# A hybrid two-layer transformer block: the first norm's order, the gates by chunks of time, and the order around three hand-overs

## The chip, the cores and the metric

The kernel runs on one core of a Trainium2 chip. A core has a matrix engine (TensorE, PE in the profile, with its weight loads as PEld), a vector engine (VectorE, DVE), an engine for activation functions (ScalarE, ACT), a general one (GpSimd, POOL) and a queue that issues most transfers (SyncE, SP). Each of them works through its own instructions in their order and waits on semaphores for the others. Matrix products are summed in PSUM, which has eight banks of 128 x 512 single-precision numbers; everything else lies in SBUF, and DRAM is reached by transfers alone. The metric is the device time of one execution in microseconds (us), lower is better.

## The reference, cut to what matters

1024 tokens `x` (the latents) and 256 tokens `ctx` (the context), both 1024 wide, go through two layers; a vector `c` modulates each norm. Everything is computed in float32.

```python
for layer in range(2):
    mod_l = silu(c) @ ada_w[layer] + ada_b[layer]        # six vectors of 1024
    mod_c = silu(c_ctx) @ ada_w[layer] + ada_b[layer]
    h_l = modulate(x, norm1_g, mod_l, 0)                 # rms_norm * (1 + scale) + shift
    h_c = modulate(ctx, norm1_g, mod_c, 0)
    # layer 0: mLSTM in both directions with gates, and window attention
    # layer 1: grouped attention of the latents over context and latents
    y_c, y_l = ab_mixer(...) if layer == 0 else c_mixer(...)
    x = x + mod_l[2] * y_l
    x = x + mod_l[5] * relu(modulate(x, norm2_g, mod_l, 3) @ w1) ** 2 @ w2
    # the context gets the same in layer 0 alone
```

The mLSTM's gates per head and direction are `log_i` and `log_f = log_sigmoid(.)`. In chunks of 128 steps the kernel needs of them the running sum of `log_f`, the running maximum `m_t`, and from these the decay of the state from chunk to chunk, the weights of the keys and `exp(-m_t)`. The scan over a chunk depends on the chunk before by one number per head only.

## The kernel before

Activations lie with their features on the 128 partitions and the tokens along the free axis, in three token groups: two of 512 latents and one of 256 context tokens (`TGS`). A float32 product is made of three products of halves: each operand is split into a rounded part and its remainder (`split`, L378 on ACT for the first and L379 on DVE or POOL for the second; for normed tokens `hhi`, L369, and `hlo`, L372 or L374), and the three matmuls hi-hi, lo-hi, hi-lo follow each other (L404 to L406 in projections, L569 in the first half of the MLP, L1020 in its second).

**First norm.** `ada_quarter` computes a quarter of the modulation's first 2048 columns: matmuls L244 with the vector `c` as the operand that stands still, then a sum over four partition groups by the matmuls L255 with `asel`. The four quarters alternate with the norm statistics of the three groups (`norm_stats`, squares summed on POOL and DVE, L315, and one matmul L300), the application of norm and modulation (`norm_apply`), and the projections of gates, window keys (L2310) and window values (`heads["v"]`, with weights in `mrv` and `irv`, L404 to L406), which take their feature tiles in the order in which the modulation has them.

**Gates.** `gates` held the 16 gate rows over all 1280 tokens: tiles of 36 partitions x 1280 columns, with four heads forward at partition 0 and four backward, reversed in time, at 32. Two scans (L1187, L1188), the logarithm of the sigmoid on ACT, exponentials of single rows (L1225, L1228), and 20 transposes (L1242) that bring the values to time on partitions. In the program it stands between the setup of the window attention (`swa_setup`: key rotation with L464 to L467 and L478) and the context's keys.

**The MLP.** The latents' two groups form a 2 x 2 block product in seven products after Strassen's scheme: `pair(b)` runs it for two tiles of hidden features, with the products `A["11"]`, `S1`, `12`, `S2`, `22`, `S3`, `S4`; L581 and L582 (`finish`) apply relu and square, L624 makes sums, and results go to DRAM (`hd`, `hc`, L584 and L600). For the context there are two direct products per pair (`direct`). The first two pairs run in `start()`. PSUM banks are handed out in turn by the list `psp.tags["A"]`. Into the pairs of layer 0 `fill(k)` puts steps of a generator (`filler`), which computes layer 1's modulation: `ada_sums`, DVE sums L209 and L211 over weights loaded at L202, and matmuls L220 over the partitions. The last pair starts `ahead()`, which loads and splits the first operands of the second half, `mlp_out`, through `mlp_feed` (loads L898, sums L943).

**mlp_out.** It takes operand pairs from a queue, one step for each hidden pair `b`, and adds its products into banks 0 to 7: in the first stage ("14") product 1 into banks 0 to 3 and product 4 into banks 4 to 7. After the second step it also loads the tokens saved before (`x<-xs`, L1088). At its end in layer 0 the context's product lies in four banks, is copied out by ACT (L1119) and transposed (L1126); the norm for layer 1 runs as a generator (`norm_steps`), and then `mixer1` splits its first weights and projects keys (`ks`, squares' matmul L1772, rotation L1775) and values.

**What sets the order.** Where nothing else is said, a scheduler places instructions by priority and its own estimates of time. Inside `manual_schedule(engines=...)` the listed engines keep the order in which the code is written.

## Time and profile before

| | |
|---|---|
| time, median of 3 runs | 2866.45 us (2858.58 to 2867.11) |
| the profiled execution | 2866.29 us, of which its span is 2864.5 us |
| mean granted clock of PE | 0.983 |
| PE idle until its first matmul | 14.1 us |
| transfers | 427.87 MB, 149 GB/s in the mean |
| PE busy in 130 to 175 us / in 175 to 250 us | 31.62 of 45 us at clock 0.77 / 73.69 of 75 us at 1.00 |

A row of a timeline gives the start and the length in us, the engine, the line of the code, the operation, the tiles it writes and reads, the shape and how many instructions were merged; in brackets stands the engine's idle time before them and whose result ended it. A row of windows gives, for a stretch, the busy time of each engine with its number of instructions, then the clock that PE was granted (1.00 is full speed), the share of the DMA engines and GB/s. A group row gives busy time, mean duration in ns, and the idle time before. SPq is the queue of SP.

### The profile page before, as it was taken

To read this page: it belongs to the slowest core of one execution; us is meant where nothing else is said; L and a number is where in the kernel's file an instruction comes from. 1 tells how busy PE (TensorE), PEld (TensorE's weight loads), DVE (VectorE), ACT (ScalarE), POOL (GpSimd) and SP (SyncE) were. 2 spreads that over 40 slices of the span, in tenths; PEclk is the share of its full clock that TensorE was granted. 3 is DMA by queue.
4 is the path that set the end of the run, shared out by engine and by line. 5 is a ranking of instruction groups with operands and counts; after the bars stand their busy time and mean duration, and the time that the engine had idled before them with its cause. 6 is when DMAs were issued, how large, how long until landed. Compare 5 with 4: busy or idle time off the path is not lost.

```text
span 2864.5 us, 41088 instructions
## 1 busy us (share of the span) xinstructions
PE 2733.7 (95%) x14806; PEld 2314.0 (81%) x14806; DVE 1996.7 (70%) x3289; ACT 1493.8 (52%) x2624; POOL 1131.6 (40%) x748
## 2 busy tenths in 40 slices
PE   6789999999999999989999998999989999999999
PEld 3678788878788878868878888999988888888877
DVE  5836556567868887756777846888885567766766
ACT  5565554444564334334345645888876555444332
POOL 3431221110227666550000335777776398840000
PEclk9989999999999999999999999999999999999999
DMA  6112224252333466669764720100026245577674
GB/s 232 61 48 95 90 88 145 96 199 89 115 103 126 165 209 214 219 209 339 249 213 156 250 88 32 34 19 27 19 83 209 86 158 195 193 254 269 212 229 155
DMA packets 193965, 427.87 MB, mean 149 GB/s; under 512 B 20960, under 2 KB 46688, under 8 KB 193760
## 3 DMA queue, kind: packets, MB, share of 16 engines
q1 hardware_dynamic: 193760, 425.24, 44.7%
q8 instruction: 116, 1.90, 0.3%
q14 instruction: 89, 0.73, 0.1%
HBM read 322.65 MB, written 102.50 MB: 148 GB/s over the span
## 4 chain that ended last, share of the span: by engine, by line
PE 67%; DVE 13%; DMA 7%; issue 5%; ACT 4%; POOL 2%; SPq 0%; DVEq 0%; POOLq 0%; ACTq 0%
PE psum L1020 15%; PE psum L569 15%; PE psum L404 5%; PE psum L406 5%; PE psum L405 5%; PE psum L1955 4%; PE psum L2141 3%; DMA hhiraw<-in_w 3%; PE psum L1861 3%; DVE W L379 2%; PE psum L1111 2%; DVE F L211 2%; DVE F L624 1%; PE psum L1453 1%; POOL W L379 1%
## 5 line engine op out<-in xcount | busy, mean ns | idle before, releaser
L379 POOL TENSOR_TENSOR W<-F,W 128x512 fp32r<-128x512 f32 (+2 forms) x323 | 522.8, 1634 | 507.8 <-ACT W L378 390.7
L1020 PE MATMUL psum<-W,W 128*128 128x512 f32 x2688 | 617.1, 391 | 8.7 <-DVE W L379 5.2
L1020 PEld LDWEIGHTS psum<-W,W 128*128 128x128 f32 x2688 | 503.9, 188 | 121.4 <-DVE W L379 12.6
L569 PE MATMUL psum<-hhi,W 128*128 128x512 f32 (+1 forms) x1600 | 448.7, 360 | 12.8 <-DVE x L624 5.9
L378 ACT ACTIVATE W<-F 128x512 fp32r<-128x512 f32 (+2 forms) x380 | 274.2, 739 | 264.5 <-POOL F L542 96.9
L569 PEld LDWEIGHTS psum<-hhi,W 128*128 128x128 f32 x1600 | 288.9, 191 | 59.1 <-DVE x L624 7.2
L569 PE MATMUL psum<-hlo,W 128*128 128x512 f32 (+1 forms) x800 | 287.2, 359 | 0.0
L378 ACT ACTIVATE W<-hhiraw 128x1024 fp32r<-128x1024 f32 x98 | 104.0, 1061 | 320.9 <-PE psum L1020 247.3
L404 PE MATMUL psum<-hhi,W 128*128 128x512 f32 (+1 forms) x624 | 232.9, 373 | 6.7 <-DVE F L478 6.7
L406 PE MATMUL psum<-hhi,W 128*128 128x512 f32 (+1 forms) x624 | 227.8, 365 | 0.4 <-POOL W L379 0.4
L405 PE MATMUL psum<-hlo,W 128*128 128x512 f32 (+1 forms) x624 | 227.5, 365 | 0.0
L943 DVE TENSOR_TENSOR hhiraw<-hhiraw 128x512 f32<-128x512 f32 x154 | 104.8, 689 | 118.2 <-DMA hhiraw<-in_w 117.4
L542 POOL TENSOR_TENSOR F<-F 128x512 f32<-128x512 f32 x112 | 170.0, 1518 | 20.4 <-DMA F<-in_w 6.9
L569 PEld LDWEIGHTS psum<-hlo,W 128*128 128x128 f32 x800 | 153.3, 192 | 21.8 <-issue 0.2
L372 POOL TENSOR_TENSOR hlo<-F,hhi 128x512 fp32r<-128x512 f32 (+1 forms) x24 | 27.9, 1165 | 358.8 <-ACT F L371 353.7
L379 DVE TENSOR_TENSOR W<-hhiraw,W 128x1024 fp32r<-128x1024 f32 x98 | 119.6, 1221 | 50.0 <-ACT W L378 49.8
L404 PEld LDWEIGHTS psum<-hhi,W 128*128 128x128 f32 x624 | 119.0, 191 | 27.6 <-DVE F L478 7.1
L406 PEld LDWEIGHTS psum<-hhi,W 128*128 128x128 f32 x624 | 118.7, 190 | 17.9 <-POOL W L379 0.8
L405 PEld LDWEIGHTS psum<-hlo,W 128*128 128x128 f32 x624 | 119.2, 191 | 16.9 <-issue 1.7
L569 PE MATMUL psum<-x,W 128*128 128x512 f32 x504 | 123.5, 389 | 0.0
L581 ACT ACTIVATE F<-F 128x512 f32<-128x512 f32 x82 | 51.2, 625 | 134.7 <-DVE F L624 134.7
L379 DVE TENSOR_TENSOR W<-hloraw,W 128x1024 fp32r<-128x1024 f32 x98 | 119.4, 1219 | 1.6 <-ACT W L378 1.6
(435 smaller groups left out, 6471.5 us busy)
## 6 DMA issues: line engine op xcount, KB each, us to landing
F<-in_w SPq DMA_DIRECT2D x104, 512.0 KB, 4.3
hloraw<-hd SPq DMA_DIRECT2D x90, 512.0 KB, 4.8
hhiraw<-in_w SPq DMA_DIRECT2D x72, 512.0 KB, 3.9
hd<-F SPq DMA_DIRECT2D x142, 256.0 KB, 2.1
hhiraw<-in_w SPq DMA_DIRECT2D x116, 256.0 KB, 5.3
F<-in_ada_w SPq DMA_DIRECT2D x96, 256.0 KB, 3.2
hd<-x SPq DMA_DIRECT2D x90, 256.0 KB, 2.4
F<-in_win SPq DMA_DIRECT2D x33, 512.0 KB, 3.7
```

The costliest lines, as they stand in the source:

```text
L378: nc.scalar.activation(hi, src, AF.Copy)
L379: eng.tensor_tensor(lo, src, hi.bitcast(F32), op=ALU.subtract)
L404: nc.tensor.matmul(ps, sh, mh, start=i == 0, stop=False)
L405: nc.tensor.matmul(ps, sh, ml, start=False, stop=False)
L406: nc.tensor.matmul(ps, sl, mh, start=False, stop=i == n - 1)
L542: add = lambda o, p, q, how: nc.gpsimd.tensor_tensor(o, p, q, op=how)
L569: nc.tensor.matmul(ps, w[i][:, p], B[j][k], start=first and j == 0 and m == 0, stop=last and j == 3 and m == 2)
L943: tt = lambda o, p, q, how: eng.tensor_tensor(o, p, q, op=how)
L1020: nc.tensor.matmul(bank(base + i), A[u][:, p], B[v], start=first and m == 0, stop=last and m == 2)
L1861: nc.tensor.matmul(ps, s[:, c], m[:, j, t0 : t0 + QT], start=j == 0 and i == 0, stop=j == ND - 1 and i == 2)
L1955: nc.tensor.matmul(u.o[:, :QT], v[x], p[y], start=c == 0 and m == 0, stop=c == 2 * NB - 1 and m == 2)
L2141: self.nc.tensor.matmul(ps, x[:, c], y, start=first and m == 0, stop=last and m == 2)
```

## The change

**First norm.** Each quarter's sum over groups takes one matmul in place of two, with the two columns of `asel` added up ahead of time. The context's tokens are loaded behind quarter 2's weights, their squares are summed by matmuls in PSUM, and all eight feature tiles of the context are normed after quarter 3. **Gates.** The gate rows go to DRAM and come back as 128 x 128 tiles: ten chunks x four heads on partitions 0 to 39 forward, 64 to 103 backward. Scans run over 128 columns; what passes between chunks is brought onto one partition row by a matmul (`across`), scanned over 80 numbers and brought back; three transposes remain, and the rows that the recurrence reads (`mr`, `ir`) go through DRAM once more. `gates` moves behind the context's keys and seven steps of the first head's gathering. **MLP.** The turns in which other work goes into `start()`, the bank order after it, the places of `fill`, the order of `ahead` and of `mlp_out`'s first two steps; the last two pairs of each layer keep the written order on all engines. **End of layer 0.** The first weights of `mixer1` are split in `mlp_out`, the keys' ahead of the four copies and the values' behind them; in layer 0 the second half of a feature tile's norm follows one tile later. **mixer1.** The order among the steps of the key groups.

```diff
+        self.asel2 = cp.tile([P, 2], F32, tag="asel2", name="asel2")
+        nc.vector.tensor_tensor(self.asel2, self.asel[:, 0:2], self.asel[:, 2:4], op=ALU.add)
...
-            for u in range(2):
-                nc.tensor.matmul(
-                    pt[:, 2 * i : 2 * i + 2], acc[:, i * P : (i + 1) * P], self.asel[:, 2 * u : 2 * u + 2],
-                    start=u == 0, stop=u == 1,
-                )
+            nc.tensor.matmul(pt[:, 2 * i : 2 * i + 2], acc[:, i * P : (i + 1) * P], self.asel2, start=True, stop=True)
...
+    def apply_first(self, g, rs, layer, which, tp, j, three=True):
+
         nc = self.nc
         t0, n, vv = g
...
+        t = tp.tile([P, 512], F32, tag="nt", name="nt", bufs=self.nt_bufs)[:, :n]
+        sh = self.shift_of(g, layer, which, j)
+        nc.vector.scalar_tensor_tensor(
+            t, self.x[j][:, t0 : t0 + n], self.gs[layer, which][:, j, vv : vv + 1], rs[:, :n],
+            op0=ALU.mult, op1=ALU.mult,
+        )
+        nc.scalar.activation(self.hhi[:, j, t0 : t0 + n], t, AF.Identity, bias=sh)
+        if j % 2 and three:
+            nc.scalar.activation(t, t, AF.Identity, bias=sh)
+        return t
...
+    def apply_second(self, g, layer, which, j, t, three=True):
...
-                turns = iter((1, 1, 1, 1, 1, 1, 4, 4) if ctx else (0, 1, 1, 2, 1, 2, 1, 2))
+                turns = iter((1, 1, 1, 2, 2, 2, 2, 3) if ctx else (0, 1, 1, 2, 1, 2, 1, 2))
...
-                turns = iter((2, 7, 1, 1) if ctx else (1, 1, 1, 1))
+                turns = iter((4, 6, 1, 1) if ctx else (1, 1, 1, 1))
...
-                        one_left(1)
+                        one_left(int(f < 3))
...
-            psp.tags["A"] = [[0, 1, 2, 3, 4, 5, 6] + ([] if ctx else [7]), 0]
+            psp.tags["A"] = [[4, 5, 6, 0, 1, 2, 3] if ctx else list(range(8)), 0]
...
-            if b == NFF // 2 - 1:
-                fill(2)
...
-            if b < NFF // 2 - 1:
-                fill(3)
+            fill(3)
...
+            if filler:
+                yield
+                yield
...
-            yield
-            yield
+            if not filler:
+                yield
+                yield
...
-            pair(b, A, nxt)
+            if b < NFF // 2 - 2:
+                pair(b, A, nxt)
+            else:
+                with self.tc.manual_schedule(engines={E.PE, E.DVE, E.Activation, E.Pool, E.SP}):
+                    pair(b, A, nxt)
...
-                if not (final and not after and b == ns - 1):
+                if stage == 0 and b < 2:
+                    if b == 0:
+                        first_two = [(*w, e, *queue[e]) for w in plan[kind] for e in range(2)]
+                    queue.popleft()
+                    work = first_two[3:] if b else first_two[:3]
+                elif not (final and not after and b == ns - 1):
...
-                    first = b == 0 and not (both and half == R)
+                    first = b + e == 0 and not (both and half == R)
...
-        for (half, i, k), y in zip(parts, ys):
-            nc.scalar.activation(y, bank(k), AF.Copy)
+        wk, wv = self.first_weights
+        wk()
+        with self.tc.manual_schedule(engines={mybir.EngineType.Activation}):
+            for (half, i, k), y in zip(parts, ys):
+                nc.scalar.activation(y, bank(k), AF.Copy)
+            wv()
...
-        for j in range(ND):
-            self.norm_apply(g, ps, layer, which, tp, [j], three)
+        if layer:
+            for j in range(ND):
+                self.norm_apply(g, ps, layer, which, tp, [j], three)
+                yield
+            return
+        t = []
+        for j in range(ND + 1):
+            if j < ND:
+                t.append(self.apply_first(g, ps, layer, which, tp, j, three))
+            if j:
+                self.apply_second(g, layer, which, j - 1, t[j - 1], three)
             yield
...
+        gd = dr.tile([4, 4, T], F32, tag="gd", name="gd")
+        for i in range(4):
+            nc.sync.dma_start(gd[i], gy[32 * i : 32 * i + 4, :])
+        for i in range(4):
+            R = (FW, BW)[i % 2]
+            nc.sync.dma_start((ig, y)[i // 2][R, :], gd[i].rearrange("h (c t) -> (h c) t", t=P))
...
-        nc.vector.tensor_tensor_scan(b, mask, f[R], 0.0, op0=ALU.mult, op1=ALU.add)
-        nc.vector.tensor_tensor_scan(m, f[R], ig[R], 0.0, op0=ALU.add, op1=ALU.max)
-        g = ig[R]
-        nc.vector.tensor_tensor(g, g, b, op=ALU.subtract)
-        nc.vector.tensor_tensor(b, m, b, op=ALU.subtract)
...
+        for R, o in ((FW, slice(None)), (BW, slice(None, None, -1))):
+            nc.vector.tensor_tensor_scan(b[R, o], z[R, :], f[R, o], 0.0, op0=ALU.mult, op1=ALU.add)
+            nc.vector.tensor_tensor_scan(m[R, o], f[R, o], ig[R, o], NEG, op0=ALU.add, op1=ALU.max)
...
+        def across(c):
+
+            ps = psp.tile("G", "gx")[:, :P]
+            nc.tensor.matmul(ps, col[:, c : c + 1].to_broadcast([P, P]), self.ident, start=True, stop=True)
+            return ps
...
+        for i, (x, dst) in enumerate(((Mh, mr), (Ml, mr), (Ih, ir), (Il, ir))):
+            for d, R in enumerate((FW, BW)):
+                w = dr.tile([4, T], F32, tag=f"gd{i}{d}", name=f"gd{i}{d}")
+                nc.sync.dma_start(w.rearrange("h (c t) -> (h c) t", t=P), x[R, :].bitcast(F32))
+                r = 64 * d + 32 * (i % 2)
+                nc.sync.dma_start(dst[r : r + 4, :].bitcast(F32), w)
...
-                mr, ir, cb, tq = self.gates(kp, small, psa, gy)
                 for _ in st[-1](psa, 0, qs):
                     pass
                 self.gps = self.banks(A=(6, 7))
                 heads = [self.gather(wp, tb, ud, h) for h in range(4)]
                 for _ in range(7):
                     next(heads[0])
+                mr, ir, cb, tq = self.gates(kp, small, psa, dr, gy)
...
+    def begin_mixer1(self):
+
+        a, wp = self.a, self.weights_ring((4, 5, 0, 1), (PG, 2 * PG, 0, 0))
+        self.wk, self.wv = [], []
+
+        def keys():
+            self.wk += [self.unit(wp, a["win1"][8 + kv]) for kv in range(2)]
+
+        def vals():
+            self.wv += [self.unit(wp, a["wv1"][:, i * 1024 : i * 1024 + 1024]) for i in range(2)]
+
+        self.first_weights = keys, vals
...
-        wk = [self.unit(wp, a["win1"][NH + kv]) for kv in range(NKV)]
-        wv = [self.unit(wp, a["wv1"][:, i * 1024 : i * 1024 + 1024]) for i in range(2)]
+        wk, wv = self.wk, self.wv
...
-                    for i in (g, g - 1, g, g - 1):
+                    for i in (g - 1, g, g, g - 1):
                         next(ks[i][kv])
             for kv in range(NKV):
+                next(ks[2][kv])
                 vals(TGS[1], (kv,))
-                for _ in range(2):
-                    next(ks[2][kv])
+                next(ks[2][kv])
...
-            if q < 3:
+            if q < 2:
                 k.load_x(a["x"], TGS[q : q + 1], 0)
-                rs[q] = k.norm_stats(TGS[q], tp, ps, "N")
             if q == 0:
+                rs[0] = k.norm_stats(TGS[0], tp, ps, "N")
                 w = [k.unit(wp, a["win0"][u]) for u in (U_G, U_KB)]
                 hl = [kp.tile([P, T], F32R, tag=x, name=x + "v")[:, :PG] for x in ("mr", "ir")]
                 heads["v"] = k.unit(wp, a["win0"][U_VB], place=(k.F[:, 7 * PG : 8 * PG], *hl))
             k.ada_quarter(q, tp, ps)
+            if q == 1:
+                rs[1] = k.norm_stats(TGS[1], tp, ps, "N")
+            if q == 2:
+                k.load_x(a["x"], TGS[2:], 0)
             todo = [(i, 2 * q, 2 * q + 2) for i in range(min(q, 2))]
-            if q < 3:
+            if q < 2:
                 todo.append((q, 0, 2 * q + 2))
-            else:
-                todo.append((2, 6, 8))
+            elif q == 3:
+                todo.append((2, 0, 8))
             for i, j0, j1 in todo:
+                if i == 2:
+                    nps = ps.tile("N", "nps")
+                    for x in k.sum_steps(TGS[2], tp, nps):
+                        pass
+                    rs[2] = k.norm_rms(TGS[2], tp, nps, x)
                 k.norm_apply(TGS[i], rs[i], 0, 1, tp, range(j0, j1))
...
+    k.begin_mixer1()
```

On DVE, in front of the window attention, the rows of the rotation of the context's keys (L464 to L467, L478; names KL, KH are the split keys) before, with the gates' rows of 36x1280 between them:

```order
L1187 SCALAR_TENSOR_TENSOR x_809<-s6f,x_812 36x1280
L464 TENSOR_TENSOR F<-F 128x256
L1188 SCALAR_TENSOR_TENSOR x_810<-x_812,x_807 36x1280
L465 SCALAR_TENSOR_TENSOR F<-psum,F 128x256
L1190 TENSOR_TENSOR x_807<-x_807,x_809 36x1280
L466 TENSOR_SCALAR F<-F 128x256
L1191 TENSOR_TENSOR x_809<-x_810,x_809 36x1280
L467 TENSOR_TENSOR F<-F 128x256
L1196 COPY rmp<-x_810 36x9
L1200 TENSOR_TENSOR x_811<-x_807,x_809 36x1280
L478 SCALAR_TENSOR_TENSOR F<-psum,vec,F 128x256
```

The same five steps now (L475 to L478, L489):

```order
L475 TENSOR_TENSOR F<-F 128x256
L1211 TENSOR_SCALAR x_1102<-x_1102 128x128
L476 SCALAR_TENSOR_TENSOR F<-psum,F 128x256
L1212 SCALAR_TENSOR_TENSOR x_1102<-x_1102 128x128
L477 TENSOR_SCALAR F<-F 128x256
L478 TENSOR_TENSOR F<-F 128x256
L1214 TENSOR_TENSOR x_1102<-x_1102 128x128
L489 SCALAR_TENSOR_TENSOR F<-psum,vec,F 128x256
```

Three rows of the gates, a tenth as wide, stand where six stood. On PE, the place of the last modulation block's matmuls in the last pair of layer 0 (W_103 holds the operand of its second product, before):

```order
L569 MATMUL psum<-hlo,W_103 128x512
L569 MATMUL psum<-hhi,W_103 128x512
L220 MATMUL psum<-ones,F 128x2 x4
L569 MATMUL psum<-hidA,W_103 128x512
L569 MATMUL psum<-hb,W_103 128x512
```

and now, where W_106 is the operand of the third product and the rows of 256 columns are the context's:

```order
L580 MATMUL psum<-hlo,W_106 128x512
L580 MATMUL psum<-hhi,W_106 128x512
L222 MATMUL psum<-ones,F 128x2 x4
L580 MATMUL psum<-hhi,W_105 128x256
L580 MATMUL psum<-hlo,W_105 128x256
```

They have moved past two products of 12 matmuls each. On SP, at the end of layer 0's first half of the MLP, behind the last modulation weights and four loads of the second half (in_w are the second half's weights, hd and hc its hidden features in DRAM, xs the saved tokens), before:

```order
L600 DMA hd_14_6510<-F 128x512
L600 DMA hd_14_6510<-x_7145 128x512
L898 DMA F<-hd_0_6496 128x1024
L898 DMA F<-in_w 128x2x512
L898 DMA F<-hd_1_6497 128x1024
L600 DMA hd_14_6510<-x_7145 128x512 x2
L584 DMA hd_15_6511<-x_7145 128x512
L898 DMA F<-hd_2_6498 128x1024
L584 DMA hc_15_6527<-F 128x256
L1088 DMA x_10165<-xs_114 128x512
L1088 DMA x_10166<-xs_114 128x512
L1088 DMA x_10167<-xs_114 128x512
```

and now:

```order
L611 DMA hd_14_6492<-x_7127 128x512 x3
L1110 DMA x_10153<-xs_116 128x512
L1110 DMA x_10154<-xs_116 128x512
L1110 DMA x_10155<-xs_116 128x512
L1110 DMA x_10153<-xs_116 128x512
L595 DMA hd_15_6493<-x_7127 128x512
L595 DMA hc_15_6509<-F 128x256
L915 DMA F<-in_w 128x512 x2
L915 DMA F<-hd_0_6478 128x1024
L915 DMA F<-in_w 128x512 x2
L915 DMA F<-hd_1_6479 128x1024
L915 DMA F<-in_w 128x512 x2
```

The loads of the saved tokens, which stood behind the first loads of the second half, now stand ahead of them.

More of the change, by code (lines that the diff above doesn't have):

```diff
@@ L1203, in gates @@
[L1203 to L1210 removed]
+        nc.vector.tensor_tensor(f, ln, z, op=ALU.add)
@@ L2280, in first @@
         tp.place("raw", [x[:, :PG] for x in sl[:6]])
-        tp.place("adaacc", cuts(k.F, H, 6 * PG))
+        tp.place("adaacc", cuts(k.F, H, 6 * PG, 6 * PG + H))
         ps = k.banks(N=(0, 1, 2), G=(0, 1, 2), K=(3, 5, 6), D=(4, 7))
```

165 lines of the change are left out of this document (73 added, 92 removed).

## The prediction

> **What bounds the kernel now.** I read the page first, then PE's order of time for its idle stretches, then windows over these stretches for the granted clock. The page says that this is a TensorE kernel:
>
> ```profile
> span 2864.5 us, 41088 instructions
> PE 2733.7 (95%) x14806; PEld 2314.0 (81%) x14806; DVE 1996.7 (70%) x3289; ACT 1493.8 (52%) x2624; POOL 1131.6 (40%) x748
> PE 67%; DVE 13%; DMA 7%; issue 5%; ACT 4%; POOL 2%; SPq 0%; DVEq 0%; POOLq 0%; ACTq 0%
> ```
>
> PE is idle for 2864.5 - 2733.7 = 131 us, 14 of them before its first matmul, so a change that leaves the products alone can win from the other 117 us and from the time at a reduced clock. The stretches of PE that the change touches are these (start, length, what PE ran, and in brackets its idle time before and who ended that):
>
> ```profile
> 54.62 0.70 PE L300 MATMUL psum<-F,ones 128*128 128x256 f32 x2 [1.21 <-DVE F L315]
> 70.97 0.50 PE L2310 MATMUL psum<-hlo,W 128*128 128x512 f32 x1 [0.55 <-POOL hlo L372]
> 73.20 0.39 PE L2310 MATMUL psum<-hlo,W 128*128 128x256 f32 x1 [0.67 <-POOL hlo L372]
> 82.79 1.22 PE L2310 MATMUL psum<-hhi,W 128*128 128x512 f32 x2 [2.07 <-ACT hhi L369]
> 141.92 0.79 PE L404 MATMUL psum<-hhi,W 128*128 128x512 f32 x1 [6.66 <-DVE F L478]
> 153.84 1.12 PE L475 MATMUL psum<-F,blk 128*128 128x512 f32 x2 [0.58 <-ACT F L446]
> 159.23 0.66 PE L1242 MATMUL psum<-ident,x 128*128 128x128 f32 x2 [4.26 <-issue]
> 165.49 0.55 PE L1413 MATMUL psum<-KH,x 128*128 128x256 f32 x1 [1.64 <-DVE small L1246]
> 872.24 0.80 PE L569 MATMUL psum<-hhi,W 128*128 128x512 f32 x1 [5.45 <-ACT F L581]
> 989.56 1.86 PE L220 MATMUL psum<-ones,F 128*128 128x2 f32 x8 [3.73 <-DVE F L211]
> 1242.22 1.87 PE L220 MATMUL psum<-ones,F 128*128 128x2 f32 x8 [8.47 <-DVE F L211]
> 1274.01 0.96 PE L1020 MATMUL psum<-W,W 128*128 128x512 f32 x3 [1.97 <-ACT F L581]
> 1276.18 4.13 PE L1020 MATMUL psum<-W,W 128*128 128x512 f32 x10 [1.21 <-DVE x L624]
> 1676.13 3.31 PE L1126 MATMUL psum<-ident,F 128*128 128x128 f32 x16 [4.38 <-ACT F L1119]
> 1728.37 0.67 PE L1772 MATMUL psum<-F,ones 128*128 128x256 f32 x2 [3.10 <-DVE F L465]
> 1746.71 0.39 PE L404 MATMUL psum<-W,hhi 128*128 128x256 f32 x1 [3.60 <-DVE F L1775]
> ```
>
> A gap costs more than its length. The windows beside them (stretch, its length, busy time of each engine, granted clock, DMA) show half the clock behind each:
>
> ```profile
> 82.00:88.00 6.00, 5.20 (x11) 3.57 (x12) 6.00 (x7) 4.60 (x7) 3.05 (x2) 0.50 0.23 73
> 139.00:147.00 8.00, 5.08 (x13) 4.02 (x14) 7.91 (x8) 6.34 (x9) 3.58 (x3) 0.57 0.25 69
> 156.00:171.00 15.00, 9.89 (x42) 8.20 (x43) 6.31 (x16) 13.07 (x21) 6.29 (x5) 0.54 0.05 17
> 870.00:877.00 7.00, 4.76 (x12) 3.75 (x13) 7.00 (x8) 5.43 (x13) 6.56 (x4) 0.51 0.22 66
> 1238.00:1249.00 11.00, 6.78 (x20) 5.72 (x21) 8.18 (x11) 5.44 (x10) 2.96 (x2) 0.53 0.53 170
> 1276.00:1280.00 4.00, 3.82 (x10) 3.05 (x11) 2.60 (x3) 1.42 (x3) 4.00 (x2) 0.57 1.05 394
> 1747.00:1750.40 3.40, 3.40 (x19) 3.40 (x19) 0.43 (x1) 0.10 (x1) 0.00 (x0) 0.53 0.13 54
> ```
>
> The busy time of such a window times the share of the clock that is missing is lost: 5.08 x 0.43 = 2.2 us in 139 to 147, 9.89 x 0.46 = 4.5 in 156 to 171, 4.76 x 0.49 = 2.3 in 870 to 877, 6.78 x 0.47 = 3.2 in 1238 to 1249, 1.6 in each of the last two. Even the gap of 2.07 us at 80.72 was followed by a clock of 0.50. So I charge about 1.7 us for a gap of 2 to 4 us, on top of it.
>
> The Trainium skill ("TensorE: Matmul & The Clock Gate", Part 1: The HAM clock gate) says that the clock falls back only after at least one idle window of about 3.4 us; the 2.07 us gap does not bear that out as a bound. By that rule the two waits of under 4 us that I add below would cost 3.4 us less, and the sum would be 2824.9 in place of 2828.3.
>
> **The change part by part.** All terms are against the profiled execution's own time, 2866.29 us, which stands 0.16 us under the median shown.
>
> *First norm (40 to 100 us).* The sums over streams take 4 matmuls per quarter where they took 8. Their row, and that of one product with a full clock:
>
> ```profile
> L255 PE MATMUL psum<-asel,F 128*128 128x2 f32 x64 | 9.1, 273 | 1.8 <-DVE F L251 1.7
> 2549.88 10.41 PE L1020 MATMUL psum<-W,W 128*128 128x512 f32 x45
> ```
>
> Half of 9.1 is 4.6 us, of which the first two quarters' share lies in a stretch where PE waits for weights anyway, so 2.3 count. The context's squares move behind quarter 2, and its 48 products of 256 columns go between those of the value projection, so that the waits of 1.21, 0.55 and 0.67 us (2.4 together) have other matmuls in front of them: the value projection's, at 10.41/45 = 0.23 us each, 72 of them. With 2 us of half clock saved that makes 7. What could hide it: the 2.07 us gap stays, since quarter 3's modulation still stands right before the last tiles. Bounds: 2 (only the halved sums) to 10 (the 2.07 gap and its clock too). **7.**
>
> *Gates (120 to 171 us).* DVE worked its 36x1280 rows between the steps of the key rotation, for which PE waited:
>
> ```profile
> 131.06 0.39 DVE L464 TENSOR_TENSOR F<-F 128x256 f32<-128x256 f32 x1
> 131.38 2.81 DVE L1188 TENSOR_TENSOR_SCAN x<-x,x 36x1280 f32<-36x1280 f32 x1
> 141.40 0.47 DVE L478 SCALAR_TENSOR_TENSOR F<-psum,vec,F 128x256 f32<-128x256 f32 x1
> L1242 PE MATMUL psum<-ident,x 128*128 128x128 f32 x20 | 4.1, 354 | 4.3 <-issue 4.3
> L1237 PE MATMUL psum<-x,ident 128*128 128x10 f32 x16 | 2.8, 308 | 0.2 <-ACT x L1228 0.2
> ```
>
> The chain L464 to L478 took 10.8 us of which its own five steps, at 0.39 to 0.47 us, are about 2 us. After, the rows between them are 128x128; the trace has none of those, and by width (a tenth of 1280) one is between 0.15 and 0.3 us. Gone are the gap of 6.66, and the 0.58, 4.26 and 1.64 us behind it, whose releasers are the old gates' transposes and copies: 13.1 us. With them go 2.2 + 4.5 us of half clock. The old gates' matmuls were 4.1 + 2.8 us; the new are six, about 2 us at the same 0.35 each, which saves 5, but most of these ran at half clock and are counted there: 2. I take off 2 for waits of the rotation itself that come out behind them. Sum 13.1 + 6.7 + 2 - 2 = **20**, bounds 12 (the rotation's chain still late by half) and 25.
>
> *Gates' pieces inside the window attention.* The three sums across chunks and three transposes stand in PE's row between the next head's projections, and the chain from the first pair to the third is some 30 small DVE rows and three ACT ones, at 0.2 to 0.3 us 8 to 9 us. PE has 18 products (18 x 0.23 = 4.1 us) and four short ones before it needs the result. That is a wait of up to 4 us and its clock. The 16 transfers of the results stand on SP ahead of gather writes and weight loads, but what they bring is needed only by the chunk recurrence, hundreds of us later. Bounds -10 and 0; nearest to the count of rows: **-4**.
>
> *Bank order behind start() of layer 0.* The 5.45 us at 866.79 waited for a bank that the last context drain (L581) held; after, the first three banks are 4, 5, 6, which are free. 5.45 + 2.3 = 7.8. PE then comes earlier to 985.83, where it waited 3.73 us for DVE's sums L211, and DVE does not come earlier; part returns there. Bounds 1 to 8: **6**.
>
> *Final modulation block and the last two pairs of layer 0.* The gap of 8.47 us at 1233.75 and 3.2 of clock. The matmuls behind it move 24 products of full width later, 24 x 0.23 = 5.5 us, and what the written order does to the block's loads on SP, which stand behind other pairs' stores, I leave between the bounds. Bounds 5.5 and 11.7: **9**.
>
> *Hand-over to the output product in layer 0.* On SP the loads of x, which wait for the last pair's products, now stand before the first loads of the output stage, and the generator that splits its operands starts two steps later. Step 1's operands are due one product after the start (12 x 0.23 = 2.8 us) in place of two. The old wait was 1.97 + 1.21 + 1.6 of clock. One POOL split takes 2.4 us by the row below, a step has two and an addition. I expect a wait of some 6 us plus clock: 5 worse. Bounds -10 to 0: **-5**.
>
> *The same in layer 1*, where there is no gap now. The last split ended at 2552.98, three us after the output products began:
>
> ```profile
> 2543.53 4.79 POOL L379 TENSOR_TENSOR W<-F,W 128x1024 fp32r<-128x1024 f32 x2 [1.81 <-ACT W L378]
> 2548.84 0.62 ACT L581 ACTIVATE x<-x 128x512 f32<-128x512 f32 x1
> 2550.19 2.79 POOL L379 TENSOR_TENSOR W<-F,W 128x1024 fp32r<-128x1024 f32 x1 [1.87 <-PE psum L569]
> ```
>
> The second step is due at 2549.88 + 2.74 = 2552.6, and the written order puts ACT's part of it behind four activations (L581, L582) of 0.62 us, 2.5 us later than now: 2552.98 + 2.5 - 2552.6 = 2.9 us, and 1.7 of clock. Bounds -8 and 0, **-5**.
>
> *Copies out of PSUM at the end of layer 0.*
>
> ```profile
> 1674.05 1.06 ACT L378 ACTIVATE W<-F 128x1024 fp32r<-128x1024 f32 x1 [5.20 <-DMA F<-in_wv]
> 1675.01 2.04 ACT L1119 ACTIVATE F<-psum 128x512 f32<-128x512 f32 x4
> ```
>
> ACT had stood 5.20 us for a value weight's DMA with the four copies queued behind it. Now the copies stand ahead of that split. The gap was 4.38; what is late next are the transposes' own context drain, and the value weights, which come later. Bounds 2 to 6: **5**.
>
> *Keys of the second mixer.* The squares' matmul goes ahead of the next projection, so that DVE's chain starts up to 24 products of 256 columns earlier. Gaps 3.10 + 3.60 and 1.6 of clock, 8.3 in all; bounds 0 (DVE is the bound there) to 8: **5**.
>
> Sum: 7 + 20 - 4 + 6 + 9 - 5 - 5 + 5 + 5 = **38**, so 2866.3 - 38 = **2828.3**, own range 2812 to 2846 (the terms' bounds do not all fall on one side).
>
> **The rivals.**
>
> *The hand-overs take more.* For it: SP, POOL and ACT serve in order, and all three are moved at these places. Against: each engine is busy for less than 70%. At their lower bounds, -10, -8 and -10 for the window attention, and 1 for the bank order: 7 + 20 - 10 + 1 + 9 - 10 - 8 + 5 + 5 = 19, **2847**.
>
> *All gaps close and nothing new opens.* Upper bounds: 10 + 25 + 0 + 8 + 11.7 + 0 + 0 + 6 + 8 = 69, **2797**. Against: the 985 us wait and L1's splits.
>
> *It doesn't do what it says.* DVE remains the bound in front, since it was the releaser of half the gaps, and rotations wait for it in the same order: first norm 2, gates 5, bank order 1, keys 0, hand-overs as in the first rival: 2 + 5 - 10 + 1 + 9 - 10 - 8 + 5 + 0 = -6, **2872**, or within 0.3% (8.6 us, about what a measurement can tell from no change).
>
> *Slower: the round trip through DRAM holds SP's queue.* 24 transfers are added, 12 out and 12 in, and each inbound one waits for its outbound one. Rows of the page:
>
> ```profile
> hd<-F SPq DMA_DIRECT2D x142, 256.0 KB, 2.1
> F<-in_ada_w SPq DMA_DIRECT2D x96, 256.0 KB, 3.2
> ```
>
> If each had to land before the next, 12 x 2.1 + 12 x 3.2 = 64 us would stand ahead of the next heads' weights, and PE would wait for these: 2866.3 - 38 + 64 = **2892**. It decides from 38 + 9 = 47 us on. Against it: the order puts the reads behind five writes, not one by one. [...]
>
> **How the numbers follow.** Forecast 0.62, first rival 0.17, all close 0.08, no effect 0.07, slower 0.06. The range of 8 in 10 takes the forecast, the first rival and half of "all close": 2800 to 2862. Faster by over 0.3%: 0.62 + 0.17 + 0.08 = 0.87; within: 0.07; slower: 0.06.
>
> **What would show it.** In PE's order of time after: no idle time over 1 us before the products that follow the rotated context keys; none behind the last direct context product of layer 0; under 4 us before the final modulation block; new gaps of 3 to 7 us at both hand-overs to the output product, and 2 to 5 us before the third sum across chunks. A loss of the sum's biggest term would show as an idle stretch between 130 and 170 us with DVE as releaser; SP standing in the gates' transfers while PE waits for a weight would prove the last rival.

## The result and the profile after

The changed kernel takes 2829.09 us (median of 4 runs, 2826.91 to 2831.78) against 2864.67 us before (2858.58 to 2867.11): a ratio of 0.988, with a 95% interval of 0.9865 to 0.9896. That is 35.6 us less; the forecast was 2828.3 us. (The kernel before has one run more than in the table above, which moves its median by 1.8 us.) First the page of the profile after, busy times and the chain that ended last:

```profile
span 2825.1 us, 40958 instructions
PE 2716.9 (96%) x14747; PEld 2303.2 (82%) x14747; DVE 1953.8 (69%) x3299; ACT 1474.9 (52%) x2611; POOL 1114.1 (39%) x741
PE 61%; DVE 12%; DMA 6%; issue 5%; ACT 3%; POOL 3%; SPq 0%; DVEq 0%; POOLq 0%; ACTq 0%
```

The span is 39.4 us shorter (the profiled execution is the fastest of the four). PE's idle time fell from 131 to 2825.1 - 2716.9 = 108 us, that is by 22.6 us; its busy time fell by 16.8, since there are 59 matmul rows less and fewer of them run at half clock. The places of the prediction, in PE's order of time after:

```profile
131.52 0.70 PE L486 MATMUL psum<-F,blk 128*128 128x256 f32 x2 [1.58 <-ACT F L452]
143.14 0.50 PE L415 MATMUL psum<-hhi,W 128*128 128x512 f32 x1 [0.50 <-ACT F L1422]
1206.11 0.47 PE L580 MATMUL psum<-hhi,W 128*128 128x512 f32 x1 [1.73 <-DVE x L635]
1211.18 1.05 PE L222 MATMUL psum<-ones,F 128*128 128x2 f32 x8 [2.06 <-DVE F L213]
1234.63 0.79 PE L1037 MATMUL psum<-W,W 128*128 128x512 f32 x1 [4.09 <-ACT W L389]
1238.88 6.55 PE L1037 MATMUL psum<-W,W 128*128 128x512 f32 x17 [3.46 <-POOL W L390]
1246.88 3.47 PE L1037 MATMUL psum<-W,W 128*128 128x512 f32 x14 [1.46 <-POOL W L390]
1637.28 2.00 PE L1152 MATMUL psum<-ident,F 128*128 128x128 f32 x16
2511.44 3.78 PE L1037 MATMUL psum<-W,W 128*128 128x512 f32 x8 [3.06 <-POOL W L390]
```

Between 130 and 171 us no idle stretch exceeds 1.58 us where there had been 6.66 and 4.26. The transposes of the context (L1152) follow the products without a wait. The final modulation block waits 2.06 us where it waited 8.47, but a wait of 1.73 us for DVE, which the kernel before does not have, stands five microseconds ahead of it. In front of the first output products of layer 0 there are three waits, 4.09 + 3.46 + 1.46 = 9.0 us, in place of 1.97 + 1.21; in layer 1 one of 3.06 us is new. The clock in these stretches, by the windows of the profile after:

```profile
130.00:171.00 41.00, 38.97 (x203) 33.28 (x204) 11.60 (x47) 14.99 (x32) 14.06 (x10) 1.00 0.25 81
842.00:849.00 7.00, 7.00 (x34) 5.83 (x33) 7.00 (x6) 4.86 (x12) 7.00 (x6) 1.00 0.21 62
1234.00:1247.00 13.00, 7.46 (x19) 5.29 (x20) 8.12 (x5) 6.72 (x11) 11.83 (x6) 0.62 0.61 204
2504.00:2518.00 14.00, 10.94 (x35) 8.07 (x35) 9.12 (x6) 6.24 (x8) 10.59 (x5) 0.76 0.91 304
```

The front runs at the full clock and PE is busy 38.97 of 41 us; both hand-overs to the output product run at a reduced one (0.62 and 0.76).

**A table by stage** tells more than the whole time. For each kernel I took from PE's order of time when a given product begins or ends: the first product of the window attention's values (`psum<-x,VV`), the 1st, 438th and 1898th product of the MLP's first half (L569, now L580), the 112th and the last of its second half (L1020, now L1037), the end of the context's transposes (L1126, now L1152), and so on. The number is the time between two of them; "again" is a second profile of the changed kernel (run e5, 2830.62 us; it was expected within 2 us of the first at every stage).

| stage, us | before | changed | again | forecast of the difference |
|---|---|---|---|---|
| start to the first window product | 198.84 | 171.36 | 170.71 | -27 |
| to the first product of layer 0's MLP | 611.27 | 613.61 | 617.96 | +4 |
| to its 438th | 93.30 | 84.49 | 84.49 | -7.8 |
| to its 1898th | 307.63 | 309.47 | 311.79 | +1.8 |
| to the 112th output product | 88.16 | 90.00 | 90.21 | -4 |
| to the last output product | 284.64 | 280.54 | 281.43 | 0 |
| to the end of the transposes | 95.61 | 89.80 | 89.80 | -5 |
| to the first product of layer 1's MLP | 559.40 | 553.90 | 552.98 | -5 |
| that MLP's first half | 311.20 | 311.24 | 311.24 | 0 |
| to the 112th output product of layer 1 | 25.27 | 31.61 | 29.04 | +5 |
| to the last output product | 285.30 | 284.68 | 284.75 | 0 |

The two profiles of one kernel agree within 0.7 us in the front and in five stages within 0.3; in the long ones, second and fourth row, they differ by 4.4 and 2.3, at layer 1's hand-over by 2.6. So a difference of 1 us can be read in some rows, and less than 5 in others means nothing. The runs below give the spread of two more rows: eight profiles with the same front begin the first window product at 170.71 to 172.07 us, and eleven with the modulation block moved take 89.75 to 91.87 us from the 1898th product to the 112th output product.

### The profile page after: what moved, and what is told of

It reads as the page before. It is cut to its first block, busy times and chain, and to the rows that moved or that the text cites. A ratio compares the mean times of both kernels' runs of the same rounds, so it can differ in the third digit from the quotient of the medians.

```text
span 2825.1 us, 40958 instructions
## 1 busy us (share of the span) xinstructions
PE 2716.9 (96%) x14747; PEld 2303.2 (82%) x14747; DVE 1953.8 (69%) x3299; ACT 1474.9 (52%) x2611; POOL 1114.1 (39%) x741
## 4 chain that ended last, share of the span: by engine, by line
PE 61%; DVE 12%; DMA 6%; issue 5%; ACT 3%; POOL 3%; SPq 0%; DVEq 0%; POOLq 0%; ACTq 0%
PE psum L1037 16%; PE psum L580 11%; PE psum L415 4%; PE psum L417 4%; PE psum L416 4%; PE psum L2003 4%; PE psum L2189 3%; PE psum L1133 3%; DMA hhiraw<-in_w 3%; PE psum L1909 3%; DVE F L635 2%; POOL W L390 2%; DVE W L390 2%; DVE x L213 1%; DVE F L213 1%
## 5 line engine op out<-in xcount | busy, mean ns | idle before, releaser
L1037 PE MATMUL psum<-W,W 128*128 128x512 f32 x2688 | 620.2, 393 | 14.9 <-POOL W L390 8.3
L1037 PEld LDWEIGHTS psum<-W,W 128*128 128x128 f32 x2688 | 507.1, 189 | 127.7 <-POOL W L390 10.1
L580 PE MATMUL psum<-hhi,W 128*128 128x512 f32 (+1 forms) x1600 | 450.1, 361 | 10.2 <-DVE x L635 8.3
L389 ACT ACTIVATE W<-F 128x512 fp32r<-128x512 f32 (+2 forms) x380 | 273.4, 739 | 263.8 <-POOL F L553 97.7
L580 PEld LDWEIGHTS psum<-hhi,W 128*128 128x128 f32 x1600 | 290.0, 192 | 56.8 <-DVE x L635 8.0
L580 PE MATMUL psum<-hlo,W 128*128 128x512 f32 (+1 forms) x800 | 287.9, 360 | 0.0
L389 ACT ACTIVATE W<-hhiraw 128x1024 fp32r<-128x1024 f32 x98 | 103.8, 1060 | 308.6 <-PE psum L1037 204.2
L580 PEld LDWEIGHTS psum<-hlo,W 128*128 128x128 f32 x800 | 154.0, 192 | 21.6 <-issue 0.2
L580 PE MATMUL psum<-x,W 128*128 128x512 f32 x504 | 123.5, 389 | 0.0
```

Source lines behind the costliest of these rows:

```text
L389: nc.scalar.activation(hi, src, AF.Copy)
L580: nc.tensor.matmul(ps, w[i][:, p], B[j][k], start=first and j == 0 and m == 0, stop=last and j == 3 and m == 2)
L1037: nc.tensor.matmul(bank(base + i), A[u][:, p], B[v], start=first and m == 0, stop=last and m == 2)
```

## The experiments

Every kernel is the changed one with one thing (or some things in separate stages) taken back. One profile and one time each, except for the last; their times scatter as those of the changed kernel do, by some 5 us, so the stages decide.

**Gates as before, in their old place.**

```diff
+                mr, ir, cb, tq = self.gates(kp, small, psa, gy)
                 for _ in st[-1](psa, 0, qs):
...
-                mr, ir, cb, tq = self.gates(kp, small, psa, dr, gy)
```

The body of `gates`, not shown, is the old one too.

> The changed kernel with the gates of before, in their old place of the program (the small tile of chunk maxima in another pool). Theory (the gates' wide vector rows held the rotation of the context's keys, and their transposes held PE): the gap of about 6.7 us before the products behind L478 and the 4.3 us before the transposes are back, and the time is 16 to 20 us above the changed kernel, near 2847 us. Rival (half of that gain came from the first norm, which leaves DVE free earlier): 6 to 10 us above, near 2837 us.

2854.25 us, 25 above the changed kernel, and 197.11 us to the first window product: 25.8 to 26.4 more. PE's idle stretches in this kernel:

```profile
130.87 2.08 PE L486 MATMUL psum<-F,blk 128*128 128x512 f32 x2 [4.26 <-ACT F L457]
148.95 1.88 PE L1272 MATMUL psum<-x,ident 128*128 128x10 f32 x8 [4.39 <-ACT x L1260]
160.59 0.66 PE L1277 MATMUL psum<-ident,x 128*128 128x128 f32 x2 [7.53 <-ACT x L1263]
```

16.2 us of waits are back, in other lots than before. All three are ended by ACT. In front of the first, ACT itself stood 5.33 us for DVE, which had rows of the gates between the steps of the rotation; in front of the other two it worked through rows of the gates itself, all of 4 partitions:

```profile
124.17 1.48 DVE L1211 TENSOR_TENSOR x<-x,x 4x1280 f32<-4x1280 f32 x1
126.14 2.02 DVE L1214 TENSOR_TENSOR x<-x,x 4x256 f32<-4x256 f32 x1
146.34 2.56 ACT L1260 ACTIVATE x<-x 4x1280 f32<-4x1280 f32 x2
155.93 5.50 ACT L1263 ACTIVATE x<-x 4x256 f32<-4x256 f32 x8 [2.02 <-POOL x L1252]
```

The gates alone are worth nearly the whole gain of the front, more than the theory gave them.

**The new gates in the old place**, so that only their shape differs from before:

```diff
+                mr, ir, cb, tq = self.gates(kp, small, psa, dr, gy)
                 for _ in st[-1](psa, 0, qs):
...
-                mr, ir, cb, tq = self.gates(kp, small, psa, dr, gy)
```

> The changed kernel with the new gates, but called where the old ones stood, ahead of the context's keys. If the width of the rows is what counts, the time stays within 4 us of the changed kernel (2825 to 2833 us) and no gap over 2 us stands between 120 and 165 us. If the place in the program counts, the three matmuls across chunks and the transposes make PE wait there for DVE again and 6 to 12 us are lost (2835 to 2841 us).

2829.95 us. The first window product comes 4.4 us later, and 1.8 of it are back 40 products on (87.45 us in place of 89.28), since the gates' matmuls are done by then. No wait between 120 and 165 us exceeds 1.75 us; the first row is the sum across chunks:

```profile
121.97 0.85 PE L1232 MATMUL psum<-ident,gcol 128*128 128x128 f32 x4 [0.70 <-DVE gcol L1227]
147.12 0.50 PE L417 MATMUL psum<-hhi,W 128*128 128x512 f32 x1 [1.75 <-POOL W L390]
```

So the shape of the gates gains 21.4 us by the first window product (197.11 to 175.72) and 23.2 by the 40th, and the place some 3. The shape is more than the width of the rows: 17 transposes and many small rows of ACT are gone with it, and no run parts these.

**First norm in its order of before** (the halved sums over groups stay):

```diff
-            if q < 2:
+            if q < 3:
                 k.load_x(a["x"], TGS[q : q + 1], 0)
+                rs[q] = k.norm_stats(TGS[q], tp, ps, "N")
```

> The changed kernel with the first norm's order of before (context's tokens loaded and squared ahead of quarter 2, squares summed before one matmul; the halved sums over groups stay). Theory: the value projection's last product ends 4 to 8 us later, at 110 to 114 us in place of 106, and the time grows by as much, to 2833 to 2837 us. Rival (PE waits there for DVE and weights anyway, the waits only change places): under 2 us.

Neither the theory nor the rival: 2822.16 us, and the first window product comes 2.2 us earlier than in the changed kernel (169.17 us; 1.5 earlier than in its second profile). Two of this kernel's idle rows on PE:

```profile
52.17 0.70 PE L298 MATMUL psum<-F,ones 128*128 128x256 f32 x2 [1.23 <-DVE F L313]
76.49 1.22 PE L2358 MATMUL psum<-hhi,W 128*128 128x512 f32 x2 [2.06 <-ACT hhi L371]
```

The 2.06 us behind quarter 3 are there in either order. The 1.23 us of the context's statistics had gone with the new order. But the changed kernel's rows at that place have waits of their own behind quarter 2, of 1.07 and 0.84 us:

```profile
58.21 0.73 PE L2367 MATMUL psum<-hhi,W 128*128 128x512 f32 x2 [1.07 <-ACT hhi L371]
62.11 0.50 PE L2367 MATMUL psum<-hlo,W 128*128 128x512 f32 x1 [0.84 <-POOL hlo L382]
```

So the new order of the first norm costs time, 1.5 to 2.2 us here.

**Bank order and turns of layer 0's first pairs**, first one, then the other:

```diff
-            psp.tags["A"] = [[4, 5, 6, 0, 1, 2, 3] if ctx else list(range(8)), 0]
+            psp.tags["A"] = [[0, 1, 2, 3, 4, 5, 6] + ([] if ctx else [7]), 0]
```

> The changed kernel with the bank order behind the first two pairs of before (0 to 6 in place of 4, 5, 6, 0 to 3). Theory: the wait of about 5.5 us for the last context drain comes back at that place, with its half clock 8 to 9 us, and the time is near 2838 us. Rival (the other turns in the first two pairs, which drain the last context product at once, did it): less than 2 us.

2825.09 us. The stage to the 438th product takes 86.05 us in place of 84.49: 1.6 us of the 8.8 that this stage won, as the rival had it.

```diff
-                turns = iter((1, 1, 1, 2, 2, 2, 2, 3) if ctx else (0, 1, 1, 2, 1, 2, 1, 2))
+                turns = iter((1, 1, 1, 1, 1, 1, 4, 4) if ctx else (0, 1, 1, 2, 1, 2, 1, 2))
...
-                        one_left(int(f < 3))
+                        one_left(1)
```

> The changed kernel with the turns of before in layer 0's first two pairs (6 ones then 4, 4; 2, 7, 1, 1; the last context drain one step late); the new bank order stays. Since the bank order alone turned out to be worth nothing, the theory is now that the early drain of the last context product removed the 5.45 us wait: the first product behind the first two pairs then starts 6 to 9 us later against the stage before, and the time is 2835 to 2838 us. Rival (either of the two, bank order or drain, is enough, since each frees a bank): under 1 us here as well.

2832.42 us, and 85.55 us for the stage, 1.1 us. By this the rival was nearer. But a few products further on PE stands 4.92 us, which no kernel with the new turns does:

```profile
878.88 0.50 PE L580 MATMUL psum<-hhi,W 128*128 128x512 f32 x1 [4.92 <-DVE F L635]
```

Counted to the 470th product, the kernel before takes 99.05 us, the changed kernel 90.25 in both profiles, this one 98.11 and e4 91.80. So the turns are worth 7.9 of the 8.8 us, near what the theory said though at another place than it said, and at the 700th product the four kernels still lie as far apart. DVE had worked through sums of the modulation (L213) ahead of the sum that PE waits for. Bank order and turns were then taken back together, along with two parts of other stages:

> The changed kernel with four parts as before, in three stages that don't touch each other: bank order and turns of the first two pairs of layer 0; the four PSUM copies at the end of layer 0 left to the scheduler behind the value weights; the key order of the second mixer. Theory: (1) with bank order and turns both undone the 5.5 us wait is back and the stage from the first product of the MLP to its 292nd takes 64 us in place of 56.5, where either alone cost 1.0 to 1.5; (2) from the output products' end to the transposes' end 95 us in place of 89.8; (3) from there to the first product of layer 1's MLP 558 to 560 us in place of 551 to 554. Together about 18 us, near 2847 us. Rival for (1): the drain and the bank have nothing to do with it, the norm ahead did it, and the stage stays under 59 us.

2844.97 us. (1) 57.36 us to the 292nd product and 86.56 to the 438th, which is still 6.7 us under before and looks like the rival's case. Where a context drain had held PE for 5.45 us, it held it for 0.84, but the wait for DVE follows here as well:

```profile
848.61 0.50 PE L580 MATMUL psum<-hidA,W 128*128 128x512 f32 x1 [0.84 <-ACT F L592]
879.97 0.50 PE L580 MATMUL psum<-hhi,W 128*128 128x512 f32 x1 [3.46 <-DVE F L635]
```

To the 470th product it takes 97.63 us: bank order and turns are worth 7.4 of the 8.8 us. For the other 1.4 us one more edit lies in this stage, the norm's second half that follows one tile later; it was not tried alone, so that its part stays open. (2) 92.36 us to the transposes' end, 2.6 more than the changed kernel's 89.80 and 3.3 under before. The transposes waited 2.35 us in place of 4.38; the keys' weights come first here too, which may be why but was not tried. (3) 559.10 us, as before (559.40): the key order is worth its 5 to 6 us.

**The written order of the last two pairs**, off in both layers, then in layer 1 alone:

```diff
-            if b < NFF // 2 - 2:
+            if b < NFF // 2 - 2 or not ctx:
                 pair(b, A, nxt)
```

> The changed kernel with the scheduler's order in the last two pairs of both layers; the final modulation block keeps its later place. Theory (the written order costs layer 1 its 6.3 us at the hand-over, by ACT's operand split behind four activations, and brings layer 0 a part of its 5.8 us before the hand-over): layer 1's hand-over wins 6 us, layer 0's last two pairs lose 0 to 4. Rival (the split of the first two output steps over two products did it, not the written order): layer 1 unchanged.

> The changed kernel with the scheduler's order in the last two pairs of layer 1 alone. Theory: no wait for POOL's split behind the first 16 output products of layer 1, 5 to 6.5 us won there, near 2823 us. Rival (it is the early need of step 1's operands in the first two output steps): the wait of 3 us stays whoever orders the pairs.

2825.80 and 2815.73 us (the latter is some 13 us below the changed kernel, more than the stage concerned explains; the rest lies in stages that scatter). Layer 1's stage takes 25.24 and 26.05 us, where the changed kernel took 31.61 and 29.04 and before 25.27: the written order is the cause, and not the split of the first two output steps, which both runs keep. ACT's order in the changed kernel and in the run with a free layer 1:

```profile
2502.47 0.63 ACT L592 ACTIVATE F<-F 128x512 f32<-128x512 f32 x1 [2.47 <-DVE F L635]
2503.13 0.63 ACT L593 ACTIVATE F<-F 128x512 f32<-128x512 f32 x1
2503.92 0.63 ACT L592 ACTIVATE x<-x 128x512 f32<-128x512 f32 x1
2504.58 0.63 ACT L593 ACTIVATE x<-x 128x512 f32<-128x512 f32 x1
2505.12 1.99 ACT L389 ACTIVATE W<-F 128x1024 fp32r<-128x1024 f32 x2
```

```profile
2496.83 2.07 ACT L389 ACTIVATE W<-F 128x1024 fp32r<-128x1024 f32 x2
2498.80 0.61 ACT L592 ACTIVATE F<-F 128x512 f32<-128x512 f32 x1
```

The two splits that the second output step needs (L389 x2) stand behind four activations in the one and ahead of them in the other. In layer 0 the written order changes nothing: from the 1898th product to the 112th output product it takes 89.75 us without it, 90.00 and 90.21 with it.

**The hand-over of layer 0.** Two runs: one with the output product's first loads two steps earlier, one with the modulation block's matmuls at their old place. The first:

```diff
-            if filler:
-                yield
-                yield
             for k in range(2):
                 feed.load(k)
...
+            if filler:
+                yield
+                yield
```

> The changed kernel with the first loads of the output product two steps earlier in the last pair (ahead of the loads of x and the last stores on SP), and with the sums over groups of the first norm in two matmuls each again. Theory (the hand-over in layer 0 waits for these loads, which SP issued behind the last pair's stores): from the 1898th product of the MLP to the 112th output product 85 to 87 us in place of 90; layer 1 the same. The front's stage to the end of the value projection grows by 2 us or less. Rival (ACT's and POOL's splits bound it, in the written order): 89.5 us or more.

This one did not test it, since the kernel computes something else. The places of the first hidden features (5 and 6 x 1024 columns into the work area) overlap those of the last modulation block's weights and sums, so that here its matmuls read hidden features and wait for them, 18.21 us:

```profile
1227.98 1.84 PE L222 MATMUL psum<-ones,F 128*128 128x2 f32 x8 [18.21 <-DMA F<-hd]
```

The stage took 96.27 us. The two steps are what the shared place demands, and the wait can't be shortened this way. Its other part, the sums over groups in two matmuls each, showed about as expected: the first window product came 1.9 to 2.6 us later (173.28 us). The second:

```diff
             prod(ps, A["11"], B11)
+            if b == NFF // 2 - 1:
+                fill(2)
```

> The changed kernel with the final modulation block's matmuls at their old place, ahead of the second product of the last pair; the written order stays. Theory (the gap of 8.5 us moved to the hand-over when it was closed, since the output product's first operands come when SP, ACT and POOL have them): the wait for DVE's sums L213 is back with 5 to 8 us, the hand-over's waits shrink by 4 to 7 us, and from the 1898th product to the 112th output product it takes 89 to 92 us, as in the changed kernel (90.0). Rival (the two are independent): 95 to 97 us.

2829.43 us, the same as the changed kernel. The old wait is back in full, the waits behind it shrink, and the stage takes 92.68 us, 2.5 to 2.7 more than with the block moved:

```profile
1211.35 1.87 PE L222 MATMUL psum<-ones,F 128*128 128x2 f32 x8 [9.30 <-DVE F L213]
1241.97 6.95 PE L1040 MATMUL psum<-W,W 128*128 128x512 f32 x17 [3.77 <-POOL W L390]
```

Against all eleven profiles with the moved block it is 0.8 to 2.9 us. So of the 7.2 us by which the block's wait shrank (9.30 to 2.06), and its clock, some 2 arrived; the rest went to the wait of 1.73 us ahead of the block and to that for the output product's operands. SP's row in the changed kernel shows when these could come, and POOL's how long it stood for them:

```profile
1221.85 1.83 SPq L1110 DMA_DIRECT2D x<-xs  x4
1225.59 0.32 SPq L595 DMA_DIRECT2D hd<-x  x1
1226.31 0.32 SPq L595 DMA_DIRECT2D hc<-F  x1
1226.72 0.90 SPq L915 DMA_DIRECT2D F<-in_w  x2
1231.28 1.26 POOL L960 TENSOR_TENSOR F<-F 128x512 f32<-128x512 f32 x1 [11.15 <-DMA F<-in_w]
```

Behind POOL's sum come ACT's split (1232.57 us) and PE (1234.63). In e11 SP issues the same loads 2.2 us later, at 1228.92 us. That the loads bound the hand-over is read from this chain; no run moved them alone.

**The two losing parts taken back together**: first norm as before, layer 1 free.

> The changed kernel without the two parts that cost time in the runs so far: the first norm in its order of before (with the halved sums over groups kept), and the scheduler's order in the last two pairs of layer 1. Theory (the two stages don't touch each other, so that what was measured in each adds up): 2 to 3 us won by the window attention's first product, 5 to 6 us at layer 1's hand-over, 2820 to 2823 us, a ratio to the kernel before of 0.984 to 0.987. Rival (the gains of single runs were scatter of the stages between): 2826 to 2831 us, as the changed kernel.

2818.94 us (median of 5, 2817.42 to 2824.37), ratio to the kernel before 0.9844, interval 0.9831 to 0.9857, which lies below that of the change. The first window product begins at 169.56 us and layer 1's stage takes 25.86, as in the single runs; the time is 1 us under the range of the theory. This is the fastest version measured with an interval, some 10 us below the change.

## Why the prediction was right, and where its terms were not

The time was right, 2829.09 us against 2828.3, and the biggest term was right in place. That it came so near was luck: the hand-over of layer 0 missed by 5.8 us one way, and the output products of layer 0, for which there was no term and whose row scatters by some 5 us, came out 4.1 us shorter.

- **Front, 27 forecast, 27.5 measured, but split wrongly.** I gave 7 to the first norm and 20 to the gates. The runs give the gates 25.8 to 26.4 (e1), above the term's upper bound of 25, the halved sums 1.9 to 2.6 (e10; 2.3 forecast) and the norm's new order -1.2 to -2.2 (e3, e12). The step that failed was to count the 1.21, 0.55 and 0.67 us of the context as gone because other matmuls stand there: waits of 1.07 and 0.84 us took their place. The gates' term was too small in both its main parts: e1 has 16.2 us of waits, where 13.1 were counted and 2 taken off, and an estimated 9 us lost by half clock (worked out at the end), where 6.7 were counted.
- **Gates' pieces in the window attention, -4 forecast.** The wait of up to 4 us before the third sum across chunks did not come: the longest near it is 0.86 us, and the first 40 window products take 89.28 us as before (89.31). The term was 0 there; the stage to the MLP grew by 2.3 and 6.7 us in two profiles of one kernel, which can't be told from scatter.
- **Bank order, 6 forecast.** The stage won 8.8, but the step that gave the cause, three free banks, failed: the bank order is worth 1.6 alone (e4), and the turns, for which no term stood, 7.9 (e6, to the 470th product). Nor did the next modulation block give back what was taken off for it: its wait is 3.58 us in the first profile and 4.69 in the second, against 3.73 before. The row below in the table, 1.8 and 4.2 us longer, lies between 305 and 315 us in all these runs and can't tell.
- **Final block and hand-over of layer 0, +9 and -5 forecast, +4 in all.** Measured: the block's wait closed as forecast, to 2.06 us, but the stage grew by 1.8 us. With the block in its old place (e11) the stage is 4.5 us above before, so the -5 was about right; it is the +9 that failed, since moving the block is worth 0.8 to 2.9 us there. The two terms were added, but they lie on one path, and behind the block PE meets the operands, whose first loads SP issues at 1226.72 us. The new waits were forecast at 6 and were 9.0.
- **Layer 1's hand-over, -5 forecast.** -6.3 and -3.8; the wait was worked out as 2.9 us and is 3.06 and 3.15, by the mechanism named (ACT's split behind four activations).
- **Copies, 5 forecast: 5.8. Keys, 5 forecast: 5.5 and 6.4.** Both places as said; but with the copies' order taken back 3.3 of the 5.8 us stay (e9), so that the order itself is worth 2.6. Of the 3.10 and 3.60 us of the keys one wait of 3.48 remains.

The rival with the round trip through DRAM fell: SP issued all 16 transfers of the results between 167.95 and 174.58 us, in 5.25 us of its own time, and PE did not wait.

The Trainium skill ("TensorE: Matmul & The Clock Gate", Part 1: The HAM clock gate) lets the clock fall back only after an idle window of about 3.4 us. Layer 1's single wait of 3.06 us, in a window at a clock of 0.76, does not bear that out as a bound, as the 2.07 us did not before the change. But the same wait of 3.15 us in the second profile passed at full clock:

```profile
2510.00:2524.00 14.00, 10.85 (x47) 8.40 (x46) 9.47 (x7) 7.24 (x9) 10.66 (x5) 1.00 0.91 306
```

That accounts for the difference between 31.61 and 29.04 us in this stage. The charge of 1.7 us lies between the two, 0 and 2.6.

## What to carry to other kernels

Price a row by what stands in line behind it: the old gates' rows of 4 to 36 partitions, up to 2.81 us each, on DVE and ACT cost PE over 20 us, since each step of another chain had to pass some of them. End a stage where two kernels run in step again: a few products behind the end first chosen, a stage that had lost 1.1 us had lost most of 7.9. Two waits on one path are not two terms: closing the first buys only what the second leaves, so look for what is late next before adding. And fix an order by hand only where the scheduler's has been seen to be worse; here the same lines that did nothing in one layer cost 4 to 6 us in the other.

## What was not expected of the hardware

The first surprise is how much time waits cost by the clock. In the run with the old gates PE was busy 27.36 us of the 41 from 130 to 171 us at a mean clock of 0.67:

```profile
130.00:171.00 41.00, 27.36 (x109) 21.66 (x109) 26.91 (x42) 32.68 (x46) 14.96 (x10) 0.67 0.04 17
```

PE was idle for 41 - 27.36 = 13.6 us of it, and some 27 us (twice 0.33 x 41) passed at half clock. By the mean clock this cost an estimated 27.36 x 0.33 = 9 us of work: two thirds of the waits themselves on top of them.

The second is that one and the same wait has no fixed price. Ten profiles with the written order have the wait in layer 1, at 3.06 to 3.53 us. In two of them (e5, e6) the clock stays full, and the stage takes 29.0 us. In four (e1, e2, e9, e11) it is halved for 3.41 us, and the stage takes 30.5 to 31.1 us; in the other four (the first profile, e3, e4, e10) for 6.83 us, and it takes 31.6 us. What decides between them was not tried.
